# Second head staged ahead of the fourth head's q and k, another order of the products behind the third sum, and a later trace of the fourth head's v and gate

## The chip, the core and the metric

The kernel runs on one core of a Trainium2 chip. The metric is the device time of one launch in microseconds (us). The core has five engines that each take their own list of instructions strictly in the order in which it was written at compile time: TensorE (PE in the profile; its weight loads are PEld), VectorE (DVE), ScalarE (ACT), GpSimd (POOL) and SyncE (SP). SP and POOL issue the DMA transfers of this kernel. An instruction that waits holds up everything behind it on its engine.

## The reference, cut to what matters

One layer of an encoder block on x of 512 tokens by 1024 channels, all in float32. What is left out here are the feed-forward half behind it and the last norm, which the change does not touch.

```python
proj = rmsnorm(x, g_mix) @ w_in
xc, gb, gc, q, k, v, g_sw, gate_a, gate_r = split(proj)
# mixer A: gated convolution over three tokens
y_a = (gb * conv3(gc * xc)) @ w_a_out
# mixer B: retention, 4 heads, q and k of 256, v of 512
scores = (rotary(q) * 256**-0.5) @ rotary(k).T * decay     # forward and backward decay in one table
ret    = group_norm_per_head(scores @ v) * g_ret
y_r    = (ret * silu(g_sw)) @ w_r_out                      # w_r_out is 2048 x 1024
merged = sigmoid(gate_a) * y_a + sigmoid(gate_r) * y_r
x      = x + merged @ w_o
```

## The kernel before, in words

Every float32 product is made of three float32r products: an operand is split into a high part, a CAST on ACT, and a low part, a subtraction on DVE (`split`, L215 and L216). So a weight tile of 128x1024 that was loaded by DMA (`raw`) costs one CAST to `whi` and one TENSOR_TENSOR to `wlo` before PE may use it. The tiles `whi` and `wlo` come from a pool of five, `raw` from a pool of ten, the 128x2048 tiles `big` from a pool of fourteen, and the accumulators of 128x512 (`bank`) from a pool of eight.

Large products use a Strassen-like scheme with seven products on sums of blocks ("forms"). For the output product y_r of the retention, heads 0 and 1 (rows 0 to 1023 of `w_r_out`) go through that scheme, and heads 2 and 3 are added with plain products (`token_major`, 48 matmuls of 512 columns for a half of the output columns of one head). The forms of the weights are b11, b21, t1 to t4 and b22; some of them are sums that are formed by DVE (L321) or by an accumulating DMA from POOL (L335). The forms of the tokens are `a11`, `a12` (made by `first_forms`), `s1`, `s2` (`sum_forms`), `s3`, `s4` and `a22` (`last_forms`). They are made from two staged tiles that hold heads 0 and 1 turned round: `stage_t(h, ...)` makes four transposes of 128x512 on DVE and then 16 DMA writes of 64 KB on SP. `do_t(h, ...)` does the same for heads 2 and 3 with eight half transposes and 16 writes, and `split_t` then splits the turned tile with the gain.

One head is handled in this way: `load_qk` and `load_v` bring q, k, v and the gate `sg` from DRAM by SP, `do_scores` multiplies and splits the scores, `split_v` splits v, and `do_pv` multiplies scores and v, normalises each bank on DVE, POOL and ACT and multiplies by the gate. Between the heads stand the products of mixer A (`mix_x`, `mix_c`, `mix_b`), and behind `mix_b(3)` follow `z_forms(3)`, which makes the forms for the product with `w_a_out` and stores them to DRAM through POOL (tensors `z020` to `z113`), and later `load_z(0)` to `load_z(3)`, which bring them back.

Three things set the order. The function `plan()` lists the weight blocks in the order in which PE will use them, and loads and splits are queued ahead in that order. The scheduler of the tile framework, which runs when the kernel is built, writes each engine's list from the traced program by its own estimates of when operands are there. And `tc.issue_after(x)` puts what is traced in its block behind the instruction x on the same engine.

In the last part of mixer B the products of before follow one another as: scores and v of head 3 (`do_pv(3)`), head 2 into the columns 512 to 1023, `s1`, `s2`, `s3`, `a22`, `s4`, head 3 into the columns 512 to 1023, head 2 into the columns 0 to 511, head 3 into the columns 0 to 511, and then the product with `w_a_out`. Behind `s2` and `s3`, `leave(o)` copies two banks to SBUF on ACT and subtracts them on DVE. `s3` goes on in the banks that `s2` filled, so it starts once these copies are made.

Of the kernel before, what the change touches and what calls it, by code (L numbers as in the profile page):

```python
# [24 lines left out]
VD = 512  # L25
# [38 lines left out]
def plan():  # L64

    out = []

    def a(name, col):
        out.append(("c", name, 0, 8, col, 256))

    def b(name, row, nk, col, nc):
        out.append(("c", name, row, nk, col, nc))

    def quad(c0, c1):
        for name in FORMS:  # L80
            for u in (0, 2):
                out.append(("q", ("w", c0, c1), name, u, 2))

    for h in range(EARLY):
        for r in (0, 512):
            b("w_in", r, 4, (C_Q + h * QK, C_K + h * QK), 512)
    for h in range(HEADS):
        quad(C_V + h * VD, C_G + h * VD)
        if h >= EARLY:
            a("w_in", C_Q + h * QK)  # L90
            a("w_in", C_K + h * QK)
    for c in (0, 512):
        quad(C_GA + c, C_GR + c)
    for c0, c1 in ((C_XC, C_GC), (C_XC + 256, C_GC + 256), (C_GB, C_GB + 256)):
        for name in FORMS:
            out.append(("q", ("x", c0, c1), name, 0, 4))
    for s in (2, 3):
        for c in (C_XC, C_GC, C_GB):
            a("w_in", c + s * 256)
    def r(*names):  # L100
        for name in names:
            for u in (0, 2):
                out.append(("q", ("r",), name, u, 2))

    r(*EARLY_FORMS[:2])
    b("w_r_out", 2 * VD, 4, 512, 512)
    r(*EARLY_FORMS[2:])
    for h, c in ((3, 512), (2, 0), (3, 0)):
        b("w_r_out", h * VD, 4, c, 512)
    for kind, name in [("a", x) for x in FORMS[:6]] + [("o", "b11"), ("a", "b22")] + [  # L110
            ("o", x) for x in ("t1", "t2", "b21", "b22", "t3", "t4")]:
        for u in (0, 2):
            out.append(("q", (kind,), name, u, 2))
    def f(q, *names):
        for n in names:
            if q == LONE:
                out.append(("q", ("f", q), n, 0, 4))
            else:
                for u in (0, 2):
                    out.append(("q", ("g", q), n, u, 2))  # L120

    def d(q0, n):
        names = FORMS if q0 + n == NQ else EARLY_FORMS
        units = [(name, u) for name in names for u in range(0, n, 2)]
        if q0 + n == NQ:

            i = units.index(("b21", 2))
            units[i:i + 3] = units[i + 1:i + 3] + units[i:i + 1]
        for name, u in units:
            out.append(("q", ("d", q0), name, u, min(2, n - u)))  # L130

    f(0, "b11", "b21")
    f(1, "b11")
    f(0, "t2", "t1", "t3", "t4", "b22")
    f(1, "t1", "t2", "b21", "t3", "t4", "b22")
    f(2, *FORMS)
    d(*FF_PARTS[0])
    f(3, *FORMS)
    f(4, *FORMS)
    d(*FF_PARTS[1])  # L140
    f(LONE, *FORMS)
    d(*FF_PARTS[2])
    return out
# [39 lines left out]
def block_kernel(ctx: ExitStack, tc: tile.TileContext, xw0, xw, xT, xtok, wpack, wquad, cols, decs, gret_rows, rot, g_ffn, g_final, out):  # L183
# [728 lines left out]
    def load_qk(h):  # L912
        tab = misctile(896, "tab")
        nc.sync.dma_start(tab, tabs[h])
        return [load(t, F32R) for t in qkd[h]], tab

    def load_v(h):
        v, sg = load(vd[h], F32R), load(sgd[h])
        if h < 2:
            g = t512()  # L920
            nc.sync.dma_start(g, gret_rows[:, 512 * h:512 * h + 512])
            return v, sg, g
        return v, sg, None
# [10 lines left out]
    def do_scores(qk, tab):  # L934
        p = (bigtile(F32R), bigtile(F32R))
        for mb in range(NB):
            ps = bank()
            for d in range(2):
                sl = slice(mb * P, (mb + 1) * P)
                mm3(ps, (qk[0][:, 2 + d, sl], qk[1][:, 2 + d, sl]), (qk[0][:, d, :], qk[1][:, d, :]),  # L940
                    d == 0, d == 1)
            t = t512()
            o = (3 - mb) * P
            nc.vector.scalar_tensor_tensor(out=t, in0=ps, scalar=QK ** -0.5, in1=tab[:, o:o + 512],
                                           op0=ALU.mult, op1=ALU.mult)
            split(t, p[0][:, mb, :], p[1][:, mb, :])
        return p
# [7 lines left out]
    def do_pv(p, vv, sg):  # L955

        for nb in range(NB):
            ps = bank()
            sl = slice(nb * P, (nb + 1) * P)
            for mb in range(NB):  # L960
                mm3(ps, (p[0][:, mb, sl], p[1][:, mb, sl]), (vv[0][:, mb, :], vv[1][:, mb, :]),
                    mb == 0, mb == NB - 1)
            st = small.tile([P, 6], F32, tag="bnst", name="bnst")
            mv = small.tile([P, 4], F32, tag="bnmv", name="bnmv")
            nc.vector.bn_stats(st, ps)
            nc.vector.bn_aggr(mv[:, 0:2], st)
            nc.vector.tensor_scalar_add(mv[:, 2:3], mv[:, 1:2], EPS)
            power = nc.gpsimd.tensor_tensor(out=mv[:, 3:4], in0=mv[:, 2:3], in1=mhalf[:, 0:1], op=ALU.pow)
            if nb == NB - 1:

                for _ in range(4):
                    sum_step(power, "heads")
            t = sg[:, nb, :]
            nc.vector.scalar_tensor_tensor(out=t, in0=ps, scalar=mv[:, 0:1], in1=t,
                                           op0=ALU.subtract, op1=ALU.mult)
            nc.scalar.activation(t, t, AF.Copy, scale=mv[:, 3:4])

    def do_t(h, t):
        yr = (bigtile(F32R), bigtile(F32R))
        transpose(lambda b: yr[1].bitcast(F32)[:, b, :], t, True)  # L980
        return yr
# [9 lines left out]
    def stage_t(h, t):  # L991
        transpose(lambda b: st["x"][b // 2][:, h, b % 2], t)
# [85 lines left out]
    v, sg2, _ = load_v(2)  # L1078
    do_pv(p, vv, sg1)
    p = do_scores(*qk)  # L1080
    qk = load_qk(3)
    vv = split_v(v)
    stage_t(1, sg1)
    c = mix_c(3, us)

    v, sg3, _ = load_v(3)
    do_pv(p, vv, sg2)
    p = do_scores(*qk)
    vv = split_v(v)
    yr2 = do_t(2, sg2)  # L1090
    mix_b(3, c, first_forms)

    a, b = ([bank(), bank()] for _ in range(2))
# [18 lines left out]
    ysum.append(bigtile())  # L1112

    def leave(o):
        for tt, u in enumerate([snap(x) for x in a]):
            nc.vector.tensor_tensor(out=ysum[1][:, o + tt, :], in0=d[tt], in1=u, op=ALU.subtract)
    leave(0)
    sgr = [bigtile(), bigtile()]
    for x, src in zip(sgr[::-1], grd[::-1]):
        load_turned(nc.sync, x, src)  # L1120
    prod_tm(4, rf["s3"], a, False)
    leave(2)
    split_t(3, yr3)
    prod_tm(4, rf["a22"], a, False)
    load_z((0,))
    prod_tm(4, rf["s4"], e, False)
    load_z((1,))

    def gate_out(half, nb, ps, add):
        t = ysum[half][:, nb, :]  # L1130
# [4 lines left out]
    token_major(yr3, e + c, old, new)  # L1135
    for nb, ps in enumerate(e + c):
        gate_out(1, nb, ps, True)
    load_z((2,))
    b = [bank(), bank()]
    token_major(yr2, b + a, [True, True, False, False], old)  # L1140
    load_z((3,))
    token_major(yr3, b + a, old, new)
    for nb, ps in enumerate(b + a):
        gate_out(0, nb, ps, nb < 2)
# [537 lines left out]
```

## Time and profile before

| | |
|---|---|
| median of 3 runs | 1024.25 us (1023.77 to 1024.36) |
| profiled execution | 1024.72 us, of which the span of the profile is 1022.9 us |
| PE busy | 1001.6 us, 98% of the span |
| DVE, ACT, POOL busy | 876.9, 554.5, 161.0 us |
| DMA traffic | 226 GB/s over the span, HBM |

In the rows of the profile, the form is engine, line, operation, output<-input, shape and count. In a timeline the first number is the start in us from the begin of the span and the second the length from the first start to the last end of the group; a bracket shows how long the engine had been idle before it and what released it. Matmuls of 128x512 overlap in the pipeline: each row shows about 0.39 us, but one starts every 0.227 us at full clock. PEclk is the granted clock as a share of the full one.

### The profile page before, as it was taken

The numbers are of one execution on the slowest core, as the hardware profiler recorded it, in microseconds if no ns is written. First come the engines' busy times: TensorE is split into PE (matmuls) and PEld (weight loads), VectorE is DVE, ScalarE is ACT, GpSimd is POOL, SyncE is SP. The second block draws the span as 40 slices with busy tenths as digits, with TensorE's granted clock in tenths as the row PEclk, the third lists the DMA queues.
The fourth block names the chain that finished last, engine by engine and source line by source line (L and its number), as shares of the span: only waits on it lengthen the run. The fifth ranks groups of instructions, "written<-read, shape, count | busy, mean of one in ns | idle before, by whom it ended". The sixth has DMA issues, their size and how long they took to land.

```text
span 1022.9 us, 13415 instructions
## 1 busy us (share of the span) xinstructions
PE 1001.6 (98%) x4722; PEld 836.8 (82%) x4722; DVE 876.9 (86%) x1141; ACT 554.5 (54%) x745; POOL 161.0 (16%) x256
## 2 busy tenths in 40 slices
PE   9999999999999999999798999999999999999996
PEld 7888888888888998888676888888888888888885
DVE  7878998979798988967886487999989996999897
ACT  7547655553655455433444334668665555564655
POOL 0030221222112004132122020011001001003202
PEclk9999999999999999999999999999999999999998
DMA  9525587694767657989758996457676459496953
GB/s 353 188 83 184 174 294 220 208 314 154 255 196 235 254 204 252 385 283 262 212 169 210 324 341 214 144 185 226 185 232 140 165 191 261 116 255 119 266 150 103
DMA packets 65795, 222.70 MB, mean 218 GB/s; under 512 B 10240, under 2 KB 10368, under 8 KB 61632
## 3 DMA queue, kind: packets, MB, share of 16 engines
q1 hardware_dynamic: 46816, 149.46, 43.2%
q0 software_dynamic: 18624, 72.10, 26.9%
q8 instruction: 37, 0.61, 0.2%
q10 hardware_dynamic: 288, 0.29, 0.1%
q14 instruction: 30, 0.25, 0.1%
HBM read 173.83 MB, written 57.41 MB: 226 GB/s over the span
## 4 chain that ended last, share of the span: by engine, by line
PE 91%; DMA 4%; DVE 2%; issue 1%; SPq 1%; POOL 0%; ACT 0%; POOLq 0%; ACTq 0%; DVEq 0%
PE bank L454 60%; PE bank L410 8%; PE bank L376 6%; PE bank L375 6%; PE bank L374 6%; PE bank L399 3%; SPq L239 1%; DMA big<-sg 1%; DMA raw<-wquad 1%; DMA big<-v 1%; DMA big<-turned 0%; PE bank L510 0%; DMA t_o<-t_o 0%; PE bank L1225 0%; PE bank L1171 0%
## 5 line engine op out<-in xcount | busy, mean ns | idle before, releaser
L215 ACT CAST whi<-raw 128x1024 fp32r<-128x1024 f32 (+2 forms) x305 | 307.9, 1029 | 237.3 <-PE bank L454 86.6
L216 DVE TENSOR_TENSOR wlo<-raw,whi 128x1024 fp32r<-128x1024 f32 (+2 forms) x306 | 358.2, 1190 | 89.4 <-ACT whi L215 84.8
L454 PE MATMUL bank<-whi,xform 128*128 128x512 f32 x1056 | 330.5, 390 | 0.0
L454 PE MATMUL bank<-whi,big 128*128 128x512 f32 x708 | 225.5, 395 | 10.4 <-ACT t L461 5.1
L454 PEld LDWEIGHTS bank<-whi,xform 128*128 128x128 f32 x1056 | 198.0, 188 | 42.1 <-DVE xform L216 1.0
L454 PE MATMUL bank<-wlo,xform 128*128 128x512 f32 x528 | 205.7, 390 | 0.0
L454 PEld LDWEIGHTS bank<-whi,big 128*128 128x128 f32 x708 | 134.8, 191 | 40.2 <-ACT t L461 5.5
L454 PE MATMUL bank<-wlo,big 128*128 128x512 f32 x354 | 139.5, 394 | 0.1
L321 DVE TENSOR_TENSOR raw<-raw 128x1024 f32<-128x1024 f32 x116 | 136.9, 1198 | 0.7
L454 PEld LDWEIGHTS bank<-wlo,xform 128*128 128x128 f32 x528 | 99.1, 188 | 21.2 <-DVE wlo L216 0.7
L461 ACT COPY t<-bank 128x512 f32<-128x512 f32 x101 | 58.8, 587 | 76.9 <-PE bank L454 62.7
L374 PE MATMUL bank<-big,whi 128*128 128x512 f32 x220 | 85.7, 390 | 0.0
L376 PE MATMUL bank<-big,wlo 128*128 128x512 f32 x220 | 85.6, 389 | 0.0
L375 PE MATMUL bank<-big,whi 128*128 128x512 f32 x220 | 85.6, 389 | 0.0
L454 PEld LDWEIGHTS bank<-wlo,big 128*128 128x128 f32 x354 | 67.5, 191 | 14.6 <-DVE wlo L216 0.6
L410 PE MATMUL bank<-xform,whi 128*128 128x256 f32 x304 | 55.3, 283 | 0.2 <-ACT t L461 0.2
L335 POOL DMA_DIRECT2D raw<-wquad x20 | 17.7, 883 | 212.4 <-ACT t L461 66.4
L375 PEld LDWEIGHTS bank<-big,whi 128*128 128x128 f32 x220 | 41.3, 188 | 8.6
L374 PEld LDWEIGHTS bank<-big,whi 128*128 128x128 f32 x220 | 41.3, 188 | 8.6
L376 PEld LDWEIGHTS bank<-big,wlo 128*128 128x128 f32 x220 | 41.3, 188 | 8.5
L410 PEld LDWEIGHTS bank<-xform,whi 128*128 128x128 f32 x304 | 47.5, 192 | 0.7 <-ACT t L461 0.6
L410 PE MATMUL bank<-xform,wlo 128*128 128x256 f32 x152 | 43.0, 283 | 0.0
(217 smaller groups left out, 1292.9 us busy)
## 6 DMA issues: line engine op xcount, KB each, us to landing
raw<-wquad SPq DMA_DIRECT2D x148, 512.0 KB, 5.2
raw<-wpack SPq DMA_DIRECT2D x34, 512.0 KB, 6.0
raw<-wquad POOLq DMA_DIRECT2D x20, 512.0 KB, 6.6
big<-turned SPq DMA_DIRECT2D x112, 64.0 KB, 4.9
t_g<-wquad POOLq DMA_DIRECT2D x12, 512.0 KB, 8.0
z<-t POOLq DMA_DIRECT2D x24, 256.0 KB, 4.8
t_o<-wquad POOLq DMA_DIRECT2D x12, 512.0 KB, 8.4
zform<-z POOLq DMA_DIRECT2D x6, 1024.0 KB, 11.6
```

The lines of the kernel that those rows point to most:

```text
L215: first = (round or nc.scalar.copy)(hi, src)
L216: low_of[0] = nc.vector.tensor_tensor(out=lo, in0=src, in1=hi.bitcast(F32), op=ALU.subtract)
L239: nc.sync.dma_start(out(b)[32 * q:32 * q + 32], ts[q // n][32 * b:32 * b + 32, q % n * 512:(q % n + 1) * 512])
L321: nc.vector.tensor_tensor(out=t, in0=t, in1=raws[quad, more, u][:, 0:n], op=ALU.add)
L335: nc.gpsimd.dma_start(out=t[:, 0:n], in_=src[:, 0:n], accum_op=ALU.add)
L374: nc.tensor.matmul(ps, lh, rh, start=first, stop=False)
L375: nc.tensor.matmul(ps, lh, rl, start=False, stop=False)
L376: nc.tensor.matmul(ps, ll, rh, start=False, stop=last)
L399: nc.tensor.matmul(pss[nb], l, r, start=start[nb] and kk == 0 and i == 0, stop=stop[nb] and kk == 3 and i == 2, skip_group_check=True)
L410: nc.tensor.matmul(o, l[:, c], r[:, k], start=start and s == 0 and k == 0 and i == 0, stop=stop and k == 3 and i == 2, skip_group_check=True)
L454: nc.tensor.matmul(pss[tt], l, r[:, c], start=start and k == 0 and i == 0, stop=stop and k == n - 1 and i == 2, skip_group_check=True)
L461: nc.scalar.copy(t, ps)
```

## The change

It has five parts.

1. In `plan()` the blocks of y_r behind t3 are listed in another order: b22, then head 2's columns 0 to 511, then t4, then head 3's columns 512 to 1023 and 0 to 511. Before it was t3, t4, b22, head 3's columns 512 to 1023, head 2's columns 0 to 511, head 3's columns 0 to 511.
2. The products follow that list: `s3`, `s4`, head 2 (columns 0 to 511), `a22`, head 3 twice. Head 2's columns 0 to 511 take two new banks and the pair of banks that `s3` has left. `load_z(0)` follows `s4`, `load_z(1)` follows `split_t(3)`, and `load_z(2)` and `load_z(3)` stand together behind head 3's first half.
3. `leave` makes both copies and returns the second; `split_t(3)` is put behind the second copy of `s3` by `issue_after`.
4. `stage_t(1)` is traced before `load_qk(3)` and `split_v(2)` and no longer behind them.
5. The loads of head 3's v and gate are traced separately: v behind `do_pv(2)`, the gate behind `do_t(2)`, and `do_t(2)` ahead of `split_v(3)`.

```diff
-    r(*EARLY_FORMS[:2])
+    r("b11", "b21")
     b("w_r_out", 2 * VD, 4, 512, 512)
-    r(*EARLY_FORMS[2:])
-    for h, c in ((3, 512), (2, 0), (3, 0)):
-        b("w_r_out", h * VD, 4, c, 512)
+    r("t1", "t2", "t3", "b22")
+    b("w_r_out", 2 * VD, 4, 0, 512)
+    r("t4")
+    for c in (512, 0):
+        b("w_r_out", 3 * VD, 4, c, 512)
...
     p = do_scores(*qk)
+    stage_t(1, sg1)
     qk = load_qk(3)
     vv = split_v(v)
-    stage_t(1, sg1)
     c = mix_c(3, us)
 
-    v, sg3, _ = load_v(3)
     do_pv(p, vv, sg2)
+    v = load(vd[3], F32R)
     p = do_scores(*qk)
+    yr2 = do_t(2, sg2)
+    sg3 = load(sgd[3])
     vv = split_v(v)
-    yr2 = do_t(2, sg2)
     mix_b(3, c, first_forms)
...
     def leave(o):
-        for tt, u in enumerate([snap(x) for x in a]):
+        us = [t512(), t512()]
+        copies = [nc.scalar.copy(u, x) for u, x in zip(us, a)]
+        for tt, u in enumerate(us):
             nc.vector.tensor_tensor(out=ysum[1][:, o + tt, :], in0=d[tt], in1=u, op=ALU.subtract)
+        return copies[-1]
     leave(0)
...
     prod_tm(4, rf["s3"], a, False)
-    leave(2)
-    split_t(3, yr3)
+    last = leave(2)
+    prod_tm(4, rf["s4"], e, False)
+    load_z((0,))
+    b = [bank(), bank()]
+    token_major(yr2, b + a, [True, True, False, False], old)
+    with tc.issue_after(last.ins):
+        split_t(3, yr3)
+    load_z((1,))
     prod_tm(4, rf["a22"], a, False)
-    load_z((0,))
-    prod_tm(4, rf["s4"], e, False)
-    load_z((1,))
...
     for nb, ps in enumerate(e + c):
         gate_out(1, nb, ps, True)
-    load_z((2,))
-    b = [bank(), bank()]
-    token_major(yr2, b + a, [True, True, False, False], old)
-    load_z((3,))
+    load_z((2, 3))
     token_major(yr3, b + a, old, new)
```

The first place at which the lists of the engines differ is ACT around `first_forms`, which makes the tiles `big_4572` that the first product `a11` reads. `big_4503` and `big_4531` are the high part of head 3's v, `t_4464` and the like (here `t512_4466`, `t512_4604` and so on) are tiles of 128x512 or half of it, `t512_4606`, `t512_4618`, `t512_4624` and `t512_4630` the high parts that `z_forms(3)` stores. Before:

```order
L215 CAST t512_4606<-big_4289 128x256
L215 CAST whi_4660<-raw_4293 128x1024
L215 CAST big_4457<-t512_4466 128x512
L215 CAST big_4457<-t512_4477 128x512
L215 CAST big_4457<-t512_4488 128x512
L215 CAST big_4457<-t512_4499 128x512
L215 CAST big_4503<-big_4365 128x1024 x2
L215 CAST big_4572<-big_3920 128x1024 x2
L215 CAST t512_4606<-big_4289 128x256
L215 CAST whi_4694<-raw_4690 128x1024
```

And now (lines are two higher in the changed kernel):

```order
L217 CAST t512_4606<-big_4289 128x256
L217 CAST whi_4660<-raw_4293 128x1024
L217 CAST whi_4694<-raw_4690 128x1024
L217 CAST t512_4606<-big_4289 128x256
L217 CAST t512_4618<-t512_4604 128x512
L217 CAST t512_4624<-t512_4605 128x512
L217 CAST t512_4630<-big_4289 128x256
L217 CAST big_4531<-big_4453 128x1024 x2
L217 CAST big_4572<-big_3920 128x1024 x2
```

The casts of `first_forms` and of head 3's v stand now behind all casts of `z_forms(3)`, where they stood ahead of the second half of it; the four casts of the scores have moved further ahead, in front of the first row. On DVE the low part of `first_forms`, `big_4573`, has moved in the same way:

```order
L873 TENSOR_TENSOR big_4289<-bank_4578,big_4289 128x512
L847 TENSOR_TENSOR t512_4604<-big_4289 128x256
L218 TENSOR_TENSOR wlo_4695<-raw_4690,whi_4694 128x1024
L218 TENSOR_TENSOR t512_4607<-big_4289,t512_4606 128x256
L847 TENSOR_TENSOR t512_4605<-t512_4604,big_4289 128x256
L847 TENSOR_TENSOR t512_4605<-big_4289,t512_4605 128x256
L218 TENSOR_TENSOR t512_4619<-t512_4604,t512_4618 128x512
L218 TENSOR_TENSOR t512_4625<-t512_4605,t512_4624 128x512
L218 TENSOR_TENSOR t512_4631<-big_4289,t512_4630 128x256
L218 TENSOR_TENSOR big_4453<-big_4453,big_4531 128x1024 x2
L218 TENSOR_TENSOR big_4573<-big_3920,big_4572 128x1024 x2
```

The first row is the multiplication of the second bank of `mix_b(3)`. Before, the four low parts of the scores, the two of v and the two of `first_forms` followed directly on that row. The tile `t512_4631` is written into the buffer that held `t512_4606`, which the first store of `z_forms(3)` reads; that store is issued by POOL behind the second cast to `t512_4606`, and the row waits until it has landed.

The second place is ACT around the copies of `s2`, the tiles `t512_5010` and its fellow. Before:

```order
L215 CAST whi_4993<-raw_4640 128x1024
L215 CAST whi_5026<-raw_3697 128x1024
L215 CAST whi_5042<-raw_3949 128x1024
L461 COPY t512_5010<-bank_4636 128x512
L461 COPY t512_5012<-bank_4637 128x512
L215 CAST whi_5072<-raw_4658 128x1024
L215 CAST whi_5090<-raw_4688 128x1024
L461 COPY t512_5058<-bank_4636 128x512
L461 COPY t512_5060<-bank_4637 128x512
```

And now:

```order
L217 CAST whi_4993<-raw_4640 128x1024
L217 CAST whi_5026<-raw_4658 128x1024
L217 CAST whi_5042<-raw_4688 128x1024
L1119 COPY t512_5010<-bank_4636 128x512
L1119 COPY t512_5011<-bank_4637 128x512
L217 CAST whi_5068<-raw_5064 128x1024
L217 CAST whi_5072<-raw_5065 128x1024
L1119 COPY t512_5058<-bank_4636 128x512
L1119 COPY t512_5059<-bank_4637 128x512
L217 CAST whi_5108<-raw_3697 128x1024
L217 CAST whi_5114<-raw_3949 128x1024
```

`raw_3697` and `raw_3949` hold t4, which POOL's accumulating DMA completes; their casts have moved from ahead of the copies of `s2` to behind the copies of `s3`. In their place stand the casts of `raw_4658` and `raw_4688`, which are b22, a plain load.

## The prediction

> **What bounds the kernel now.** I read the page first, then PE's waits and a table by stretches, and last the timelines of PE, ACT, DVE, POOL and SP around the places these named.
>
> ```profile
> span 1022.9 us, 13415 instructions
> PE 1001.6 (98%) x4722; PEld 836.8 (82%) x4722; DVE 876.9 (86%) x1141; ACT 554.5 (54%) x745; POOL 161.0 (16%) x256
> ```
>
> PE is busy from end to end, so only its few gaps can be won. The span is 1.8 us shorter than its execution, 1024.72 us, which lies 0.47 us above the median of 1024.25. PE's waits between 500 and 570 us, and the stretches there (columns: length, PE, PEld, DVE, ACT, POOL busy, clock, DMA share, GB/s):
>
> ```profile
> PE bank L454 <- ACT t L461: 5.1, 1, 5.1
> PE bank L454 <- ACT big L215: 3.1, 1, 3.1
> PE bank L454 <- DVE big L216: 2.2, 1, 2.2
> ...
> 510.00:520.00 10.00, 9.11 (x31) 7.41 (x32) 8.10 (x11) 4.31 (x7) 3.87 (x6) 0.74 0.75 225
> 530.00:540.00 10.00, 9.88 (x43) 7.55 (x42) 10.00 (x26) 3.95 (x6) 2.78 (x6) 1.00 0.00 1
> 560.00:570.00 10.00, 8.41 (x27) 6.75 (x28) 5.38 (x6) 5.00 (x7) 0.00 (x0) 0.68 1.01 383
> ```
>
> So two stalls, A at 504 and B at 556, each followed by a low clock (0.74, 0.68), are all that the change can win by removing idle time; elsewhere PE runs at 1.00 without gaps. PE's timeline gives their cost:
>
> ```profile
> 503.91 0.39 PE L376 MATMUL bank<-big,wlo 128*128 128x512 f32 x1
> 507.41 0.50 PE L454 MATMUL bank<-whi,big 128*128 128x512 f32 x1 [3.11 <-ACT big L215]
> 510.89 1.22 PE L454 MATMUL bank<-whi,big 128*128 128x512 f32 x2 [2.22 <-DVE big L216]
> 514.04 1.06 PE L454 MATMUL bank<-whi,big 128*128 128x512 f32 x2
> ...
> 556.09 0.39 PE L454 MATMUL bank<-whi,big 128*128 128x512 f32 x1
> 561.59 0.79 PE L454 MATMUL bank<-whi,big 128*128 128x512 f32 x1 [5.11 <-ACT t L461]
> 566.44 0.63 PE L454 MATMUL bank<-whi,big 128*128 128x512 f32 x2
> ```
>
> At a matmul each 0.227 us, B's s3 would have begun at 556.32 and its thirteenth matmul at 559.04; it began at 566.67 (the second of the last row). B costs 7.6 us: 5.3 of waiting, 2.4 of low clock. In the same way A's thirteenth matmul starts at 514.47 instead of 506.86 and A costs 7.6 us.
>
> **Stall B goes: −7.6 us.** ACT and POOL ahead of it:
>
> ```profile
> 556.86 1.04 ACT L215 CAST whi<-raw 128x1024 fp32r<-128x1024 f32 x1 [5.36 <-DMA raw<-wquad]
> 560.01 1.04 ACT L215 CAST whi<-raw 128x1024 fp32r<-128x1024 f32 x1 [2.10 <-DMA raw<-wquad]
> 560.96 1.07 ACT L461 COPY t<-bank 128x512 f32<-128x512 f32 x2
> ...
> 545.59 1.02 POOL L335 DMA_DIRECT2D raw<-wquad  x1
> 551.16 0.88 POOL L335 DMA_DIRECT2D raw<-wquad  x1 [4.55 <-DVE wlo L216]
> ```
>
> PE waits for the copies of s2, and these queue on ACT behind the two casts of t4, which wait for POOL's accumulating DMAs (issued 545.59 and 551.16, landed when the casts start). Now the two casts ahead of the copies are those of b22, a plain load that in before was in SBUF long before its cast. The copies then run as soon as the banks are done, the first under the second bank's six matmuls (1.36 us against a copy of 0.59). What is late next is t4, behind the copies of s3: it is wanted at `a22`, which now follows s3, s4 and head 2, 5.4 + 5.4 + 10.9 = 21.8 us behind the start of s3, over 15 us after the t4 casts of before. Behind t4 in ACT's list stand only weights and `split_t(3)` for products later still. So nothing takes B's place there, and I take the whole 7.6; the other bound is nil, if the copies are late for a reason I don't see.
>
> **The bank waits behind head 3's scores go: −0.7 us.** Head 2's first 48 matmuls take from 533.90 to 545.44, 11.54 us instead of 10.88:
>
> ```profile
> 533.90 0.39 PE L399 MATMUL bank<-whi,big 128*128 128x512 f32 x1
> 545.44 0.39 PE L454 MATMUL bank<-whi,big 128*128 128x512 f32 x1
> ...
> 539.29 2.39 DVE L236 STREAM_TRANSPOSE turned<-big 128x256 f32<-128x256 f32 x7
> ```
>
> They wait for banks that DVE normalises late, since most of `sum_forms` (ten operations of 128x512, about 0.6 each like those at 504.94 below) lies among them; DVE is busy 10.00 of 10.00 there. `sum_forms` is now wholly ahead of the first normalisation; three operations of 1.15 take its place, each between two banks that PE makes 2.7 us apart. This also brings the transposes of head 3 (row 539.29, until 541.7) forward: by the same kind of walk as below they end some 4 us sooner behind PE's scores-times-v, of which I count 2.8.
>
> **Stall A grows: +3.9 us.** This is the price. `first_forms` has moved behind all of `z_forms(3)`, whose second half needs the second bank of mix_b. I walk ACT's and DVE's new lists with the durations of the old rows:
>
> ```profile
> 502.35 2.18 ACT L215 CAST big<-t 128x512 fp32r<-128x512 f32 x4
> 504.42 3.89 ACT L215 CAST big<-big 128x1024 fp32r<-128x1024 f32 x4
> 508.21 0.40 ACT L215 CAST t<-big 128x256 fp32r<-128x256 f32 x1
> ...
> 490.20 2.70 DVE L812 SCALAR_TENSOR_TENSOR big<-u,cols_sb,big 128x512 f32<-128x512 f32 x4
> 499.24 0.65 DVE L871 TENSOR_TENSOR big<-bank,big 128x512 f32<-128x512 f32 x1
> 504.34 0.69 DVE L871 TENSOR_TENSOR big<-bank,big 128x512 f32<-128x512 f32 x1 [0.64 <-PE bank L376]
> 504.94 2.49 DVE L216 TENSOR_TENSOR big<-t,big 128x512 fp32r<-128x512 f32 x4
> 507.35 4.62 DVE L216 TENSOR_TENSOR big<-big 128x1024 fp32r<-128x1024 f32 x4
> ...
> 508.91 0.76 POOL L666 DMA_DIRECT2D z<-t  x1 [6.62 <-ACT t L215]
> ...
> DMA to landing us min/median/max: 2.8/4.6/6.8
> ```
>
> (The last row is of the eight z stores from 505 to 525 us.) The four low parts of the scores, 2.4 us, now run before the transposes of head 2, so mix_b's first multiplication moves from 499.24 to about 501.7 and the second, behind a weight's low part, from 504.34 to 504.95. Then DVE does that multiplication, six small operations and one weight, at 0.35, 0.6 and 1.15 each 4.4 us, and is free for `t512_4631` at 509.4. ACT casts the second t512_4606 (0.35), t512_4618 and t512_4624 (0.55 each, the latter at 508.2 behind DVE) and t512_4630 until 509.1, v until 511.0 and the first high part of `first_forms` until 512.0 (0.95 each). So PE's first product starts at 512.05, not 507.41.
>
> Its third matmul wants the low part. The store of t512_4606 is issued 0.3 us behind its cast, at 506.3, and lands 2.8 to 6.8 us later; t512_4631 ends at 509.75 without a wait, at 511.3 with the median of 4.6, at 513.5 with 6.8. Behind it come v's two low parts and the first of `first_forms`, 3.45 us (from 510.1 at the earliest, when v's first cast is done). PE's third matmul starts at 513.6, 514.75 or 516.9 against 510.89: +2.7, +3.9, +6.0. I take the median, because the eight writes and the gate of 1 MB that ran beside that store now come later. The low clock over the first four matmuls (1.7 us) is hidden in the wait, and over the next eight it was paid before too. A second unknown lies ahead: stage_t(1) and the loads on SP.
>
> ```profile
> 466.25 0.32 SPq L909 DMA_DIRECT2D big<-ql  x1
> 488.01 0.32 SPq L909 DMA_DIRECT2D big<-v  x1
> 490.31 12.37 SPq L239 DMA_DIRECT2D big<-big  x16
> 502.72 0.58 SPq L909 DMA_DIRECT2D big<-sg  x1
> ```
>
> The 16 writes of stage_t(1), from 490.31 before, now follow ql, which stays near 466. By the list the convolution (DVE at 490.20) waits for their landing, and the eighth write waits for ql's. The writes take 12.4 us by themselves; with some 10 us for the megabyte of ql I estimate 489, which leaves 490.20 as it is. Up to 4 us late goes one for one into A; early is worth 0.7 at most, since PE gives the second bank at 504.34.
>
> In the Trainium skill, "TensorE: Matmul & The Clock Gate" (Part 1: The HAM clock gate) says the clock halves after an idle window of about 3.4 us and comes back after one as busy. This trace agrees in size: 12 matmuls in 5.1 us after 5.1 idle. By that rule a stall under 3.4 us costs only itself; here 3.1 and 2.2 us with four matmuls between them were enough for 0.74. Either way A was low before and stays low.
>
> **The moved loads themselves: 0.** v still waits for the end of do_pv(2), as at 488.01 before, and is cast from 509 on. The gate goes behind do_t(2)'s 16 writes, from 502.72 to about 512. It is first read with head 3's first bank, which PE ends three quarters of 10.9 us ahead of 533.90, so at 525.7 and with A's growth near 530: 18 us for one megabyte. q and k have until 488, when the scores of head 3 begin.
>
> **Weights for the last products: 0.** With B gone PE wants everything behind it 8.3 us earlier, counted from the end of the scores-times-v (533.90, then E):
>
> ```profile
> 577.49 1.56 SPq L260 DMA_DIRECT2D raw<-wpack  x2
> ...
> 594.40 1.05 ACT L215 CAST whi<-raw 128x1024 fp32r<-128x1024 f32 x1 [4.60 <-DVE big L1133]
> ...
> 601.82 0.62 PE L399 MATMUL bank<-whi,big 128*128 128x512 f32 x2
> ```
>
> The tightest is the first block of the last product. In before it was issued at 577.49, cast on landing at 594.40 (E + 60.5) and used at 602.04 (E + 68.1). The block that is wanted first there now has the same place on SP, the 29th transfer from head 3's turned writes on, and is wanted at E + 59.8 (five and a half times 10.9). With the landing unchanged PE would wait 1.7 us for the cast and 2.7 in all for the low part. But SP's row of transfers begins with those writes, 2.8 us nearer to E, so the block lands at about E + 57.7, is cast at 58.7 and split at 59.9: just in time.
>
> **The sum.** 1024.72 − 7.6 − 0.7 + 3.9 = 1020.3 for a profiled execution, and 0.47 less for the median: **1019.9 us**.
>
> **The rivals.** *The late weight decides (slower).* The DMA engines are full there (1.01 at 383 GB/s from 560 to 570), and POOL's reloads of z and gate A are now released by earlier products, so they may push back SP's weights instead of these coming 2.8 us earlier. Landing at an unchanged E + 60.5 costs 2.7 us idle and up to 2.4 of low clock as in B: 1025.0. If 2 MB of reloads slip ahead, 5.2 us at that rate, and SP bears half, 2.6 us more: 1027.6. With the low clock it is slower than before by more than 0.2% from a landing at E + 61.8 on. Against it: POOL reloaded z beside SP's weights in before too. The Trainium skill has the rule in "DMA: Bandwidth & Descriptors" (Issuing engines are not separate DMA queues): transfers of all issuers interleave on the same 16 engines. No row here shows which queue gives way.
>
> *Stall A grows past the gain (slower).* Store at 6.8 us and the stage writes landing 4.5 late: +10.5 instead of +3.9, 1026.5; the point is +8.3. For it: half of the writes are held by ql's landing, which no row above fixes.
>
> *Stall A hardly grows (faster still).* The store lands before its reader and the convolution is early: +2.0, 1018.0. Under that I see no way down, since the order of the lists holds `first_forms` back whatever the DMAs do.
>
> *B only moves.* If the copies of s2 still come late, A's growth stands alone: 1024.25 + 3.2 = 1027.5. The list speaks against it.
>
> **How the numbers follow.** What I forecast has 0.55, with its own range of 1017.5 to 1023 (0.47 faster, 0.08 the same); A hardly grows 0.13 (faster); late weight 0.17 (0.02 faster, 0.08 the same, 0.07 slower); A past the gain 0.10 (0.04 the same, 0.06 slower); B moves 0.05 (slower). Faster by over 0.2% (2.05 us, about what a measurement can tell) 0.62, within 0.2% 0.20, slower 0.18. The range 1016.5 to 1026.5 leaves out the far ends of these.
>
> **What would show it.** PE's waits should have no row for the copies and no low clock behind 550 us; the one at `a11` should be near 8 us for ACT and a further wait for DVE, with t512_4631's operation on DVE standing just behind a z store's landing. Wrong would be: a PE wait at the last product (L401) for a DMA, an `a11` start before 510, or a convolution after 492.

## The result and the profile after

| | before | changed |
|---|---|---|
| median | 1024.01 us (1022.87 to 1024.36, 4 runs) | 1031.15 us (1030.13 to 1031.78, 4 runs) |
| ratio to before | | 1.0071, 95% interval 1.0053 to 1.0088 |
| profiled execution | 1024.72 us | 1030.13 us |
| span of the profile | 1022.9 us | 1028.3 us |

The change is slower by 7 us where 4 faster were predicted. PE's busy time is unchanged and the span is 5.4 us longer, so on balance what came on top is idle time of PE. The page of the changed kernel has

```profile
PE 1001.4 (97%) x4722; PEld 836.4 (81%) x4722; DVE 876.5 (85%) x1141; ACT 554.3 (54%) x745; POOL 161.0 (16%) x256
```

and PE's waits over its whole span are (engine and line, what it waited for, us in total, times, longest)

```profile
PE bank L456 <- ACT big L217: 9.7, 1, 9.7
PE bank L401 <- ACT whi L217: 4.5, 1, 4.5
...
PE bank L456 <- DVE big L218: 1.1, 1, 1.1
PE bank L401 <- DVE wlo L218: 0.5, 1, 0.5
PE bank L456 <- DVE wlo L218: 0.5, 1, 0.5
```

Stall B has no row any more, stall A has grown (9.7 and 1.1 us, before 3.1 and 2.2), and L401, the plain products of heads 2 and 3, has a wait that was not there before. The same in stretches of the changed kernel (columns as in the prediction):

```profile
510.00:520.00 10.00, 5.78 (x13) 4.10 (x14) 6.10 (x7) 5.26 (x7) 3.33 (x6) 0.50 0.88 278
560.00:570.00 10.00, 10.00 (x46) 8.28 (x45) 6.97 (x8) 5.77 (x8) 0.53 (x1) 1.00 1.02 365
600.00:610.00 10.00, 5.93 (x15) 4.37 (x16) 4.08 (x4) 3.98 (x4) 0.00 (x0) 0.66 1.03 303
```

At 560 us the clock is 1.00 where it was 0.68; the low one is now at 600. PE's timeline has both stalls and, between them, the first matmul behind the scores-times-v (E of the prediction, 533.90 before):

```profile
513.15 0.79 PE L456 MATMUL bank<-whi,big 128*128 128x512 f32 x1 [9.73 <-ACT big L217]
515.87 1.22 PE L456 MATMUL bank<-whi,big 128*128 128x512 f32 x2 [1.07 <-DVE big L218]
...
539.10 0.39 PE L401 MATMUL bank<-whi,big 128*128 128x512 f32 x1
...
603.60 0.80 PE L401 MATMUL bank<-whi,big 128*128 128x512 f32 x1 [4.50 <-ACT whi L217]
604.86 0.80 PE L401 MATMUL bank<-wlo,big 128*128 128x512 f32 x1 [0.46 <-DVE wlo L218]
...
609.14 0.63 PE L401 MATMUL bank<-whi,big 128*128 128x512 f32 x2
```

PE executes the same number of matmuls in all kernels here, so the n-th matmul of one profile can be set against the n-th of before. The difference of their starts says where time is lost or won. This table is worked out in that way from PE's timeline; the first column is when that matmul starts in before, and the kernels that follow are explained below (us, plus is later than before):

| start in before | changed | order_only | without_part5 | gate_half_later | reloads_held | no_part5_held | order_only_held | loads_only | part4_out_held | gate_only_held |
|---|---|---|---|---|---|---|---|---|---|---|
| 503.9, ahead of A | −0.9 | 0.0 | −0.6 | −1.2 | −0.9 | −0.4 | −0.7 | +0.3 | +0.1 | −0.8 |
| 522.6, behind A | +5.2 | −0.1 | −1.4 | +6.9 | +5.8 | −1.3 | −1.0 | +7.3 | +4.6 | +5.7 |
| 556.1, behind the bank waits | +4.5 | 0.0 | −2.0 | +6.3 | +5.1 | −1.9 | −0.4 | +6.6 | +3.9 | +5.0 |
| 569.4, behind B | −3.1 | −7.7 | −9.7 | −1.4 | −2.5 | −9.6 | −8.0 | +3.5 | −3.7 | −2.6 |
| 596.4 | −3.1 | −7.7 | −9.7 | −1.4 | −2.5 | −9.6 | −8.0 | +3.5 | −3.7 | −2.6 |
| 601.8, ahead of the last product | −3.1 | +4.8 | +3.0 | −1.4 | −2.5 | −7.5 | −8.0 | +3.5 | −3.7 | −2.6 |
| 607.9, in the last product | +4.7 | +4.8 | +3.0 | −1.4 | −2.5 | −7.5 | −8.0 | +3.5 | −3.7 | +1.6 |
| 626.1, in the product with w_a_out | +5.4 | +4.8 | +3.0 | +4.7 | −2.5 | −7.5 | −8.0 | +3.5 | −3.7 | +1.6 |
| 1008.4, last part | +5.4 | +5.0 | +4.0 | +5.5 | −2.0 | −7.4 | −7.6 | +3.5 | −3.7 | +1.7 |

So the changed kernel's account is: −0.9 from its first matmuls on (it is there at 25.8 us already, where the traces of the other kernels lie between −1.2 and +0.4), A +6.1, bank waits −0.7, B −7.6, the last product +7.8, the product with w_a_out +0.7. The sum is +5.4, as between the two profiled executions.

The new loss of 7.8 us is 5.0 us of waiting and, for the rest, a low clock for the next matmuls: eleven of them take from 603.60 to 609.14, 5.5 us, of which 0.5 is the second wait, instead of 2.5. What PE waits for there is the cast of the last product's first weight block, and the cast waits for the block's landing. ACT, then SP and POOL of the changed kernel:

```profile
602.50 1.04 ACT L217 CAST whi<-raw 128x1024 fp32r<-128x1024 f32 x1 [23.54 <-DMA raw<-wpack]
```

```profile
543.33 13.63 SPq L241 DMA_DIRECT2D big<-turned  x16
...
561.73 15.42 SPq L934 DMA_DIRECT2D big<-gr  x8
...
582.44 4.13 SPq L262 DMA_DIRECT2D raw<-wpack  x2
```

```profile
571.98 1.05 POOL L1054 DMA_DIRECT2D zform<-z  x2 [10.13 <-PE bank L456]
582.86 0.53 POOL L1054 DMA_DIRECT2D zform<-z  x1 [9.83 <-PE bank L401]
583.81 1.04 POOL L1054 DMA_DIRECT2D zform<-z  x2 [0.43 <-DMA big<-gr]
588.52 2.23 POOL L934 DMA_DIRECT2D big<-ga  x4 [3.67 <-PE bank L456]
```

In the trace the block landed at 602.40, E + 63.3 (before at 594.30, E + 60.4). POOL's reloads, by contrast, were issued much earlier than before, as these rows of before show:

```profile
575.30 0.53 POOL L1052 DMA_DIRECT2D zform<-z  x1 [17.56 <-PE bank L454]
580.52 1.05 POOL L1052 DMA_DIRECT2D zform<-z  x2 [4.69 <-PE bank L454]
594.71 1.05 POOL L1052 DMA_DIRECT2D zform<-z  x2 [13.15 <-DVE big L1133]
602.28 4.51 POOL L932 DMA_DIRECT2D big<-ga  x8 [6.52 <-PE bank L399]
```

Counted from E, the last two rows of before are at 60.8 and 68.4; in the changed kernel the same transfers (z3 and the first four of gate A, 1 MB each) are at 44.7 and 49.4, ahead of the block's landing instead of behind it.

### The profile page after: what moved, and what is told of

Its sections match the earlier page's. It is cut to its first block, busy times and chain, and to the rows that moved or that the text cites. A ratio compares the mean times of both kernels' runs of the same rounds, so it can differ in the third digit from the quotient of the medians.

```text
span 1028.3 us, 13417 instructions
## 1 busy us (share of the span) xinstructions
PE 1001.4 (97%) x4722; PEld 836.4 (81%) x4722; DVE 876.5 (85%) x1141; ACT 554.3 (54%) x745; POOL 161.0 (16%) x256
## 4 chain that ended last, share of the span: by engine, by line
PE 82%; DMA 8%; DVE 6%; SPq 1%; issue 1%; ACT 1%; POOL 0%; POOLq 0%; ACTq 0%; DVEq 0%
PE bank L456 56%; PE bank L412 8%; PE bank L376 5%; PE bank L377 5%; PE bank L378 5%; DMA big<-turned 2%; DMA big<-gr 2%; DMA raw<-wpack 2%; DMA big<-ql 2%; SPq L241 1%; DVE wlo L218 1%; DVE raw L323 1%; DVE turned L238 0%; DVE big L1142 0%; DVE big L218 0%
## 5 line engine op out<-in xcount | busy, mean ns | idle before, releaser
L456 PE MATMUL bank<-whi,big 128*128 128x512 f32 x708 | 224.5, 393 | 10.8 <-ACT big L217 9.7
L463 ACT COPY t<-bank 128x512 f32<-128x512 f32 x97 | 56.6, 586 | 73.9 <-PE bank L456 59.5
L401 PE MATMUL bank<-whi,big 128*128 128x512 f32 x128 | 41.8, 404 | 4.5 <-ACT whi L217 4.5
```

The source lines that it names most:

```text
L401: nc.tensor.matmul(pss[nb], l, r, start=start[nb] and kk == 0 and i == 0, stop=stop[nb] and kk == 3 and i == 2, skip_group_check=True)
L456: nc.tensor.matmul(pss[tt], l, r[:, c], start=start and k == 0 and i == 0, stop=stop and k == n - 1 and i == 2, skip_group_check=True)
L463: nc.scalar.copy(t, ps)
```

## The experiments

Each of the following kernels computes the whole layer. The kernel before was run beside them on the same chip (medians 1024.14, 1024.44 and 1024.64 us in the three groups).

**Parts of the change alone.** `order_only` is the kernel before with parts 1 to 3, `without_part5` the change with part 5 undone. Both are edits of this kind:

```diff
-    do_pv(p, vv, sg2)
-    v = load(vd[3], F32R)
-    p = do_scores(*qk)
-    yr2 = do_t(2, sg2)
-    sg3 = load(sgd[3])
-    vv = split_v(v)
+    v, sg3, _ = load_v(3)
+    do_pv(p, vv, sg2)
+    p = do_scores(*qk)
+    vv = split_v(v)
+    yr2 = do_t(2, sg2)
```

(`order_only` has `stage_t(1, sg1)` behind `split_v(v)` again as well.)

> Only parts 1 to 3 of the change (the order of the products and its weights, the copies, split_t(3)); stage_t(1) and the loads of head 3's v and gate as before. Theory (the transfers that stand ahead of the last product's weights set when it starts, whatever the first part of the change does): stall A stays at the 7.6 us of before, stall B (7.6) is gone, and PE waits at the last product for a weight cast at least as long as in the changed kernel (5 us idle, 7.8 in all), since head 3's transposes start 3 us later again: a net of 0 to +3 us on the kernel before, 1024 to 1027 us. Rival (the wait at the last product is a consequence of the moved loads, parts 4 and 5): no wait there, 1016.5 us.

> Parts 1 to 4 without part 5: head 3's v and gate are loaded as before. In ACT's and DVE's lists first_forms then stands ahead of z_forms(3) and on DVE even ahead of the second multiplication of mix_b(3). Theory (part 5 alone made stall A grow, by the order of the lists): stall A costs 3 to 5 us instead of the changed kernel's 13.7, the wait at the last product stays at 7 to 9 us: about 1021 us. Rival (stall A grew because stage_t(1) was moved ahead, part 4, and its writes land late): A stays above 11 us and the time near 1030.

`order_only`: 1030.36 us (1029.69 to 1032.08), ratio 1.0065 (1.005 to 1.008). `without_part5`: 1028.6 us (1026.32 to 1032.61), ratio 1.005 (1.003 to 1.007). PE's longest waits in `order_only`:

```profile
PE bank L401 <- ACT whi L217: 9.1, 1, 9.1
PE bank L456 <- ACT big L217: 3.1, 1, 3.1
PE bank L456 <- DVE big L218: 2.2, 1, 2.2
```

and in `without_part5`:

```profile
PE bank L401 <- ACT whi L217: 8.7, 1, 8.7
PE bank L456 <- DVE big L218: 4.5, 1, 4.5
```

Three things follow. With parts 1 to 3 alone A is as before (3.1 and 2.2) and B is gone, −7.7 in the table; so the gain at B comes from the order of the products. With part 5 undone A no longer grows (PE is 0.6 early ahead of it and 1.4 early behind it, not 5.2 late), though it shrinks by 0.8 us only, to 6.8, where 3 to 5 were expected; so part 5 is needed for A's growth. And the late weight is there without parts 4 and 5, and worse: the earlier PE arrives, the earlier the block that is late. Both times lie above the theory's forecasts; that of `without_part5` comes near its rival's 1030, but not for the rival's reason, since A is 6.8 and not above 11. The theory's sign held for the late weight, its size did not: the late block is now one of head 3's columns 512 to 1023 and costs 12.4 and 12.6 us (from −7.7 to +4.8, from −9.7 to +3.0), all of the gain and 3 to 5 us more.

**The gate's first half later.** In the changed kernel the second half of `gr` on SP (1 MB in four transfers) is issued behind the last weight block instead of ahead of it.

```diff
     sgr = [bigtile(), bigtile()]
-    for x, src in zip(sgr[::-1], grd[::-1]):
-        load_turned(nc.sync, x, src)
+    load_turned(nc.sync, sgr[1], grd[1])
...
         gate_out(1, nb, ps, True)
+    with tc.issue_after(block_dma[0].ins):
+        load_turned(nc.sync, sgr[0], grd[0])
     load_z((2, 3))
```

(`block_dma[0]` is the last weight transfer traced by then.)

> The changed kernel, but the four loads of the second half of gate R (gr0, 1 MB) are queued on SP behind the last product's two weight blocks instead of ahead of them. Theory (the row of transfers ahead of these weights is what makes them late): the first block lands 6 to 8 us sooner, the 7.8 us at the last product and the 0.8 us behind it go, 1022.6 us. Rival (what delays them is POOL's reloads of z that are released earlier, and they fill whatever SP leaves free): the block lands under 3 us sooner, at least 4 us remain, 1027 us or more.

1031.22 us (1029.16 to 1033.93), ratio 1.0072 (1.005 to 1.0094). No gain, and not for the rival's reason: the block lands at E + 54.2 (595.03), 9.1 us sooner, and the wait at the last product is gone. PE's waits from 570 to 660 us now are

```profile
PE bank L457 <- issue: 2.2, 1, 2.2
PE bank L457 <- DVE wlo L218: 1.7, 1, 1.7
```

in the product with w_a_out, whose weights DVE has to sum first and which come late:

```profile
609.63 1.23 DVE L324 TENSOR_TENSOR raw<-raw 128x1024 f32<-128x1024 f32 x1 [6.24 <-DMA raw<-wquad]
```

The transfer that DVE waits for there lands at 609.54, E + 68.7, and in the changed kernel at E + 68.6; PE is only there sooner. So a loss of 6.1 us stands between 607.9 and 626.1 in the table instead of the 7.8 at the last product: it has moved. This other order on SP's queue was not enough.

**The reloads held.** In the changed kernel POOL issues the reloads of z2, z3 and gate A only when the first bank of head 3's columns 512 to 1023 has been added. A POOL addition on one column of that sum, whose result nobody reads, waits for it, and the reloads stand behind it.

```diff
         gate_out(1, nb, ps, True)
-    load_z((2, 3))
+    held = small.tile([P, 1], F32, tag="held", name="held", bufs=1)
+    with tc.issue_after(nc.gpsimd.tensor_scalar_add(held, ysum[1][:, 0, 0:1], 0.0).ins):
+        load_z((2, 3))
```

> The changed kernel, but POOL's reloads of z groups 2 and 3 and of gate A wait, by a one-column operation on POOL, until the first bank of head 3's columns 512 to 1023 is added on DVE, about 4 us later than their buffers are free for group 2 and 0 to 15 us later than in the changed kernel for the rest. Theory (pulled-forward reloads took about half of the lost time, SP's own row the other): the block lands 3 to 6 us sooner, 2 to 5 us remain at the last product, 1025 to 1028 us. Rival (SP's own row alone, eight in flight): the landing does not move, 1031 us.

1023.91 us (1022.48 to 1024.65, 10 runs), ratio 0.9995 (0.9986 to 1.0005): 7.2 us less than the changed kernel. Counted from E, the block lands 10.0 us sooner (rows below), where 3 to 6 were expected. The table has nothing left at the last product (−2.5 and −2.5), where the changed kernel lost 7.8, and nothing in the product with w_a_out. So with those reloads out of the way the whole of that loss goes, not a part. PE, ACT and DVE execute the same operations in the same order in both traces, so it is not another list that did it.

**Control: the kernel before with the same hold.**

```diff
         gate_out(1, nb, ps, True)
-    load_z((2,))
+    held = small.tile([P, 1], F32, tag="held", name="held", bufs=1)
+    with tc.issue_after(nc.gpsimd.tensor_scalar_add(held, ysum[1][:, 0, 0:1], 0.0).ins):
+        load_z((2,))
```

> The kernel before with the reloads of z2, z3 and gate A held at the same place and nothing else. Theory: the weights are in time there already (the tightest cast, at 594.40, is followed by no wait on PE), so holding gives nothing: 1024.1, 1023 to 1025. Rival: held reloads help by themselves, elsewhere than at a late weight (fewer transfers beside the full queues between 560 and 600): 1022 or less, and then part of what the held version of the change gained has nothing to do with the change.

1024.09 us (1022.65 to 1025.74, 10 runs), ratio 0.9995 (0.9986 to 1.0004). Holding is worth nothing in this kernel, where no weight is late.

**Only gate A held**, z2 and z3 as in the change:

```diff
-    for t, src in zip(sga, gad):
-        load_turned(nc.gpsimd, t, src)
+    held = small.tile([P, 1], F32, tag="held", name="held", bufs=1)
+    with tc.issue_after(nc.gpsimd.tensor_scalar_add(held, ysum[1][:, 0, 0:1], 0.0).ins):
+        for t, src in zip(sga, gad):
+            load_turned(nc.gpsimd, t, src)
```

> The changed kernel with only gate A's reloads held (to the same point); z2 and z3 as in the change. In the changed kernel four of gate A's transfers (1 MB, issued at 588.5) and z3 (1 MB, 583.8) are what POOL issued earlier, ahead of the landing of the late weight at 602.4, beyond what it had issued by then in the kernel before. Theory: transfers of the two queues share the DMA engines, so that each MB taken away brings the weight forward by about 2.8 us: landing at E + 60.5, half of the loss at the last product gone, 1027, 1026 to 1029. Rival: what is issued first is moved first; gate A is issued 6 us behind the late weight (582.4) and does not delay it: 1030.5 to 1031.5.

1028.55 us (1024.62 to 1031.16, 10 runs), ratio 1.0035 (1.002 to 1.005), where sharing gave 1026 to 1029 and first come, first served 1030.5 to 1031.5. The runs spread from the one forecast to the other, so the times do not decide. What decides is the trace of the profiled run, 1026.4 us, one of the quicker ones; the traces of the slower ones are not known. The loss at the last product falls from 7.8 to 4.3 (−2.6 to +1.6). ACT's row for the block's cast in `gate_only_held`, and then the one in `reloads_held`:

```profile
599.82 1.04 ACT L217 CAST whi<-raw 128x1024 fp32r<-128x1024 f32 x1 [19.73 <-DMA raw<-wpack]
```

```profile
593.03 1.05 ACT L217 CAST whi<-raw 128x1024 fp32r<-128x1024 f32 x1 [13.30 <-DMA raw<-wpack]
```

With E at 539.59 and 539.66, the block landed at E + 60.1 (the theory said 60.5) and E + 53.3; in the changed kernel, at E + 63.3. What the queues moved from E + 20.9 (560 us in the changed kernel) to that landing (q1 is SP's, q0 POOL's; packets, MB, share of the time of the 16 engines) is, in the changed kernel, in 42.4 us,

```profile
q0 software_dynamic: 1403, 8.18, 57.1%
q1 hardware_dynamic: 2306, 5.81, 45.5%
```

with only gate A held, in 39.2 us,

```profile
q0 software_dynamic: 1185, 7.41, 53.5%
q1 hardware_dynamic: 2337, 5.93, 49.1%
```

and with all reloads held, in 32.3 us,

```profile
q1 hardware_dynamic: 2415, 6.12, 64.0%
q0 software_dynamic: 631, 4.35, 38.8%
```

SP's queue moved nearly the same in all three, 5.8 to 6.1 MB. POOL's moved 0.77 MB less with gate A held and 3.83 MB less with all held, and the block came 3.2 and 10.0 us sooner. That is 4.1 and 2.6 us for each MB, so no single price holds. The time on the engines does add up: POOL's share is 24.2, 21.0 and 12.5 us, SP's 19.3, 19.2 and 20.7. So the block waits in full for whatever POOL's queue moves ahead of its landing, although it was issued on another queue and, for gate A, 6 us earlier: gate A's first transfer in the changed kernel, issued at 588.52, landed at 602.39, with the block that was issued at 582.44.

The Trainium skill has a rule for this in "DMA: Bandwidth & Descriptors" (Queues, rings and completion order): each DMA engine goes round the queues that have work for it, a packet at a time. The measured bytes fit it: with work on both, neither queue stands still, and what is issued later on POOL's still goes ahead of what is at the back of SP's. The turns themselves no run here shows.

**A taken apart.** `part4_out_held` is `reloads_held` with part 4 undone (stage_t(1) behind load_qk(3) and split_v(2)):

```diff
-    stage_t(1, sg1)
     qk = load_qk(3)
     vv = split_v(v)
+    stage_t(1, sg1)
```

> The changed kernel without part 4 (stage_t(1) traced behind load_qk(3) and split_v(2) again), reloads held as before. The order of first_forms behind z_forms(3) is kept. Theory: of A's growth some 2 us come from the convolution, which is held by the landing of stage_t(1)'s writes (491.9 there against 490.2 in the kernel before, 2.6 late once the earlier start of that run is taken off) and not from the order of the lists; without part 4 the writes are behind the convolution again, A falls to about +4, and the time from 1023.9 to 1021.3, 1020 to 1022.5. Rival: A is as long as the z store and the lists make it; the convolution is not what decides, and the time stays at 1023.9, 1023 to 1025.

1021.98 us (1020.94 to 1023.26, 10 runs), ratio 0.9977 (0.9968 to 0.9986); 1.9 less than `reloads_held`, 2.6 expected. A falls from 6.7 to 4.5 us (table: +0.1 to +4.6). The convolution is at 490.29 again. The first row is DVE's of the changed kernel, the second ACT's ahead of it, the third SP's with the last nine writes of stage_t(1):

```profile
491.15 2.74 DVE L814 SCALAR_TENSOR_TENSOR big<-u,cols_sb,big 128x512 f32<-128x512 f32 x4 [4.90 <-ACT big L812]
```

```profile
490.39 1.34 ACT L812 ACTIVATE big<-u,cols_sb 128x512 f32<-128x512 f32 x2 [6.05 <-DMA big<-big]
```

```profile
482.70 6.04 SPq L241 DMA_DIRECT2D big<-big  x9
```

ACT has been waiting for 6 us for the landing of those writes. PE is 0.9 early there, so the convolution is 1.8 late against 490.20 of before, and part 4 is what puts it there.

**Parts 4 and 5 alone** (the loads of the change, the products in the order of before; the diff is that of the change without its parts 1 to 3).

> Parts 4 and 5 alone: stage_t(1), v, gate and do_t(2) traced as in the change, products in the order of the kernel before. Theory: A grows by 6.1 as in the changed kernel, the bank waits give back 0.7, B stays, and as PE is then late rather than early no weight is late: 1024.1 + 5.4 = 1029.5, 1028 to 1030.5. Rival: the transfers that B waits for do not move with PE, so that PE's lateness eats into B's 5.1 us of waiting and the sum is near the kernel before: 1024 to 1026.

1027.29 us (1025.19 to 1031.12, 8 runs), ratio 1.0028 (1.0015 to 1.004), between the two. A costs 7.0 and the bank waits give 0.7 back, as expected, but B gives 3.1: PE waits for the copies of s2

```profile
PE bank L454 <- ACT t L461: 2.6, 1, 2.6
```

instead of 5.1, since PE is 6.6 us late while t4's casts, at 558.26 and 564.16, are only 1.4 and 4.2 later than before. The price of parts 4 and 5 thus depends on what is waited for behind them.

**The change without its price.** `no_part5_held` is `without_part5` with the reloads held, `order_only_held` is `order_only` with them.

> Parts 1 to 4 of the change, and POOL's reloads of z2, z3 and gate A held until the first bank of head 3's columns 512 to 1023 has been added. Theory: part 5 is what makes stall A grow, and the reloads that are released earlier are what makes the weights late; with neither, only the gain at B is left. From the trace without part 5, the matmuls ahead of the late weight start 8.5 to 9 us before those of the kernel before, so 1024.1 - 8.5 = 1015.6 us, 1014.5 to 1017.5. Rival: in this order of events the late block is an earlier one (head 3's columns 512 to 1023, at 587 us), and the reload of z1 ahead of it, which is not held, is enough to make it late: half of the 8.7 us waited there stay, 1020, up to 1024.

> Parts 1 to 3 alone (other order of the products, gate and loads as in the kernel before), with the same reloads held. Theory: stall A as in the kernel before, B gone, no late weight: 1024.1 - 7.6 = 1016.5, 1015.5 to 1018; and so within 2 us of the same without part 5 alone. Rival: z1's reload, not held, still delays the weight of head 3's columns 512 to 1023, of the 9.1 us waited there half stay: 1021 or more.

1015.14 us (1013.66 to 1017.3, 5 runs), ratio 0.9908 (0.9893 to 0.9923), and 1016.99 us (1016.4 to 1017.64), ratio 0.9922 (0.9909 to 0.9936). Both beat the kernel before by 0.8% to 0.9% and the changed kernel by 14 to 16 us. In the first, PE's waits are

```profile
PE bank L456 <- DVE big L218: 4.5, 1, 4.5
...
PE bank L401 <- DVE wlo L218: 0.8, 1, 0.8
PE bank L401 <- ACT whi L217: 0.7, 1, 0.7
```

so of the 12.6 us at head 3's columns 512 to 1023 there are 2.0 left (−9.6 to −7.5).

**z1's reload held too**, on top of `no_part5_held`:

```diff
     with tc.issue_after(last.ins):
         split_t(3, yr3)
-    load_z((1,))
...
-        load_z((2, 3))
+        load_z((1, 2, 3))
```

> As the run without part 5 with reloads held (1015.1), and z1's two reloads held as well. Theory: the 1.5 us of waiting (2.0 with the clock) left at head 3's columns 512 to 1023 come from z1's reload of 1 MB at 565.5, ahead of that weight: 1015.1 - 2.0 = 1013.1, 1012.3 to 1014.3. Rival: SP itself is late there (it waits for gr's landings), or z1 is now late for the product with w_a_out: 1015 or more.

1019.91 us (1019.63 to 1021.32, 5 runs), ratio 0.9956 (0.9944 to 0.9969): a miss for the time, though not for the place. The waits at L401 are gone and the 626.1 row is at −10.5, but from 645 us on PE loses 5.5 us in small steps. The first of them, in PE's timeline, are

```profile
650.03 0.50 PE L456 MATMUL bank<-whi,xform 128*128 128x512 f32 x1 [0.96 <-ACT xform L217]
...
693.75 1.38 PE L1231 MATMUL bank<-ident,t 128*128 128x128 f32 x8 [0.86 <-DVE t L1217]
```

There ACT's list stands in another order (casts of xform and of weights and copies out of banks change places). Whether that is the cause of this loss was not tested.

## Why the prediction was wrong, point by point

*Stall B, −7.6.* Right. B is gone in every kernel with the new order of the products, by −7.6 to −7.7 (−7.6 in the changed one). The mechanism held too: in ACT's timeline of the changed kernel the copies of s2 wait for the banks alone, and no longer for a cast of t4:

```profile
559.70 0.59 ACT L1119 COPY t<-bank 128x512 f32<-128x512 f32 x1 [0.26 <-PE bank L456]
561.06 0.59 ACT L1119 COPY t<-bank 128x512 f32<-128x512 f32 x1 [0.77 <-PE bank L456]
```

*Bank waits, −0.7.* Right: −0.7; head 2's 48 matmuls now take 10.89 us, from 539.10 to 549.99.

*Stall A, +3.9.* Right mechanism, too small: +6.1. As the prediction said, t512_4631's operation on DVE stands just behind the landing of a z store, and that store, issued at 507.27 and landed at 511.89, took the 4.6 us of the median:

```profile
511.98 0.42 DVE L218 TENSOR_TENSOR t<-big,t 128x256 fp32r<-128x256 f32 x1 [1.31 <-DMA z<-t]
```

PE's first product starts at 513.15, that is 514.0 once the 0.9 us of the earlier start is taken off, where the walk gave 512.05; the matmul that waits for the low part (the prediction calls it the third; it is the fourth here and was the fifth in before) at 515.87, or 516.75, against 514.75. Both are 2.0 later. The step that failed here is the estimate of 489 for the landing of stage_t(1)'s writes, "which leaves 490.20 as it is": it allowed some 10 us for the megabyte of ql, which took 17.0, from 465.73 to 482.69. The eighth write went out at 482.70, the last landed at 490.13, and the convolution waited until 491.15, 1.8 late, which the prediction took to go one for one into A. Without those writes ahead of it A is 4.5 and the first product starts at 511.98, as walked; the store took 6.1 us there instead of 4.6. In the other runs with parts 4 and 5 A grew by 6.5 to 8.1 us.

*Moved loads, 0.* Right as far as PE shows: nothing waits for v, the gate, or q and k.

*Weights for the last products, 0.* This is the step that failed and turned the forecast over: +7.8, and +0.7 behind it. The prediction let SP's row of transfers begin 2.8 us nearer to E and took the landing to move with it, to E + 57.7. SP did begin earlier, at E + 4.2 (543.33) instead of E + 7.5, as this row of before shows:

```profile
541.42 14.37 SPq L239 DMA_DIRECT2D big<-turned  x16
```

But the lead was gone when the block was issued, at E + 43.3 instead of E + 43.6. SP issues a transfer in these traces only when the one eight places ahead has landed (the block was issued at 582.44, that transfer landed at 582.38), and with POOL's transfers beside them these had lost their lead. The landing itself came 2.9 us later, at E + 63.3. The changed kernel's 8.18 MB of POOL's queue and 5.81 of SP's from E + 20.9 to the landing, 24.2 and 19.3 us of the engines' time, stand against these in before, 19.3 and 21.4 us of 39.5:

```profile
q1 hardware_dynamic: 2479, 6.12, 54.2%
q0 software_dynamic: 1054, 6.94, 48.9%
```

The reloads had been released by PE's earlier products, as the rival said. What the prediction named as the sign of its being wrong, a wait at L401 for a DMA, is there by way of the cast.

*The rivals.* "The late weight decides" was right, with 0.17. It put a landing of E + 63.1 and a loss of 7.7 for 2 MB of reloads that slip ahead, and the loss was 7.8; but it reached this with SP bearing half of the 2 MB and no earlier start, while the runs show a start that was earlier and a block that bears the whole, from POOL's 1.24 MB more ahead of the landing. So its mechanism was right, and that 7.7 came so near to 7.8 was luck. Its time of 1027.6 lacked A's further 2.2, the 0.7 in the product with w_a_out, and 0.6 that is neither: the median lies 1.0 above the profiled execution, not 0.5 below it, and the profiled run started 0.9 early. "A grows past the gain" did not decide: with the late weight removed and A as it was, the time is that of before (1023.91). "B only moves" was wrong: B went, and the new wait has another cause.

*The range.* Its upper end, 1026.5, rested on one mishap at a time. Here two came together, A at +6.1 and the late weight at +8.5.

## What to carry to other kernels

Before counting a removed stall as a gain, look at what the stall paid for: between 560 and 605 us the DMA engines are busy all the time (a share of 1.01 to 1.07 in every 5 us of the changed kernel), so PE's gain of 7.6 us only brought it sooner to weights that came later. A transfer that is released by progress of PE comes sooner when PE does, and while the engines are full, what waits on the other queue is pushed back by all the time it takes, whoever was issued first; so give a reload that is wanted late an explicit release point behind the loads that are wanted first. Doing this for z2, z3 and gate A, and taking out part 5, turned the change from 7 us lost into 9 us won.

## What the runs showed of the hardware

A transfer on POOL's queue delays one that was issued 6 us earlier on SP's by its whole time on the engines: with 3.2 us less of POOL's ahead of it (0.77 MB) the block landed 3.2 us sooner, and with 11.7 us less (3.83 MB) and 1.4 us more of SP's, 10.0 us sooner. A stall costs more than its wait: 5.0 us of waiting at the last product went with a clock of 0.66 over 600 to 610 us and 2.8 us more. In `gate_only_held`, the loss of 4.3 us was twice the waiting of 1.3 and 0.8:

```profile
PE bank L401 <- ACT whi L217: 1.3, 1, 1.3
PE bank L401 <- DVE wlo L218: 0.8, 1, 0.8
```
